# Four head pairs in the seven-product output projection, with weight sums made by accumulating transfers

## The chip, the cores and the metric

The kernel runs on one core of a Trainium2 chip. The metric is the device time of one execution in microseconds. The kernel before took 963.85 us (median of 3 runs, 963.8 to 965.16).

## The reference

One layer of a hybrid decoder, over 512 tokens and 16 learned meta tokens, model width 2048, all in float32:

```python
h = rms_norm(x, norm_w)
proj = (h @ w_in).astype(f32)
(dq, dk, dv, dz, db, da, gq, gk, gv, gz, gl, fq, fk, fv, fz, ff) = split_cols(proj)
...
o_dn = gated_head_norm(gated_delta_rule_chunked(...), dz, dn_norm_w)    # 6 heads x 128
o_gla = gated_head_norm(gla_chunked(...), gz, gla_norm_w)               # 5 heads x 128
o_fox = forgetting_attention(...) * silu(fz)                            # 5 heads x 128
o = jnp.concatenate([o_dn, o_gla, o_fox], axis=-1)[:, PAD:]
return x + o @ w_out          # then a final RMSNorm, meta tokens dropped
```

The output projection is `o @ w_out`: 512 tokens, 16 heads of 128 (eight head pairs `kp` 0 to 7), 2048 columns (four blocks `cc` of 512).

## The kernel before

Every matmul operand is split into a high and a low part, and a product is three matmuls: high by high, high by low, low by high. The program has three phases.

The first phase (about 93 to 490 us) is the input projection. Column blocks are taken in 18 pairs (`Pair`), and a pair is computed with seven products in place of eight (PE tile `px`). SyncE loads the raw weights `a`, VectorE makes their sums, ScalarE casts each operand to its high part `hp`, VectorE subtracts to get `lp`. Both have three buffers, and each operand of 128x1024 feeds 24 matmuls. Results that are needed later are spilled to DRAM. Beside it, the masks of DeltaNet (`an`, ten blocks) are loaded, cut with an AFFINE_SELECT on GpSimd and go into a triangular inverse (`inverse`, tile `ab`, on VectorE), whose result goes through a DRAM scratch `sc` and comes back as `xc`, transposed as `uc`, for the PE product `pm`.

The middle (490 to 817 us) runs the three mixers beside the rest of the input projection (`pbgz`, `pbfq`, `pbfz`, products of 512 columns) and the first part of the output projection (`po`). GLA's scores inside a chunk are `pss`: bursts of tiny matmuls of 64 and 32 rows, for the heads in pairs.

The last phase (817 us to the end) is the output projection. `PLAN` gives its order on PE. `OUT` holds plain products of head pairs 0 to 2. `Seven(cp)` does the column blocks 2cp and 2cp+1 with seven products for the head pairs in `ST`, here 3, 4 and 6 (PE tile `ps`). A set of seven products needs seven weight operands for each head pair: three raw quarters (numbers 1, 2, 3) and four sums (5, 7, 6, 4), and the same for the heads. `seven_raws` loads the quarters, `seven_sums` makes the sums on VectorE, `seven_operands` splits them into `wh` and `wl`, `seven_heads` does the heads, and `seven_adds` adds each product to the accumulator `acc` in SBUF. `late` holds the plain products of the head pairs not in `ST`, 5 and 7, for column blocks 0 to 2; `mm_last` takes the last column block, with head pairs 2, 5 and 7, one row block (128 tokens, `tb`) after the other, starting from `acc` (PE tile `pz`); each finished row block is normalised and sent out as 1 MB. The last row block goes in two halves. The order is late, Seven(0), late, Seven(1), late, last block.

What sets the order of the work is `Weave`, a list scheduler that runs when the kernel is built. Each piece of work is a generator with a priority; a cost model (`cost`) gives every instruction a duration, and the scheduler emits the instruction that could start first. That fixes the order of instructions on each engine. `BACK` says how far ahead of the model's clock of the DMA queues a load is asked for. The model changes no times on the chip, but every change in costs or work moves instructions everywhere behind it. SyncE issues nearly all transfers, in order; an instruction that waits holds what is behind it on its engine.

## Time and profile before

| | us |
|---|---|
| median of 3 runs | 963.85 |
| profiled execution | 968.62 |
| its span | 966.6 |
| TensorE busy in it | 949.7 |
| VectorE busy | 753.4 |
| ScalarE busy | 559.6 |
| GpSimd busy | 38.8 |

The profile shows one execution. Its span leaves out 2.0 us around the recorded instructions. A busy share is a mean over stages with different limits, so what a stage is worth is read from its own window and from the chain of work that ended last. PE records overlap, since matmuls are pipelined: a matmul of 128x512 has a duration of about 0.39 us and a start 0.23 us behind the one ahead of it. A wait "<-issue" is one for which the profile shows no other work or transfer that ended it.

### The profile page before, as it was taken

Reading aid. Unit: us, or ns where it says so; the run is one execution under the profiler, and the core shown is the slowest. Engines: PE = TensorE matmul, PEld = TensorE weight load, DVE = VectorE, ACT = ScalarE, POOL = GpSimd, SP = SyncE. Lnnn points to the kernel's source line nnn. Section 1 sums busy time; section 2 is a strip of 40 time slices with the busy share of each in tenths; the row PEclk is TensorE's granted clock in tenths of the full one; section 3 lists DMA queues with packets and bytes.
Section 4 is the critical chain, followed back from the end, with each engine's and each line's share of the span. In section 5 each row is a group of like instructions: output and inputs, shape, how many; then the busy total and the mean of one; then the engine's idle time right before and its main releaser. Section 6 shows DMA issues by size and latency. Waiting matters only on the chain.

```text
span 966.6 us, 18894 instructions
## 1 busy us (share of the span) xinstructions
PE 949.7 (98%) x7301; PEld 847.1 (88%) x7301; DVE 753.4 (78%) x1346; ACT 559.6 (58%) x1192; POOL 38.8 (4%) x86
## 2 busy tenths in 40 slices
PE   9999999999999999999999999989999999999996
PEld 7888999999999999999987897768787887888885
DVE  7986888888888788888983676866867976889874
ACT  7865566667756575654423775647555664335534
POOL 0000000000000000000000021001010100000000
PEclk9999999999999999999999999999999999999999
DMA  9933235426542545542188444324244246733105
GB/s 340 360 132 132 88 121 168 159 94 188 146 162 89 157 125 173 157 147 85 62 312 269 129 124 144 132 79 143 79 135 157 83 142 205 285 98 120 44 23 174
DMA packets 78894, 144.10 MB, mean 149 GB/s; under 512 B 14781, under 2 KB 35005, under 8 KB 78804
## 3 DMA queue, kind: packets, MB, share of 16 engines
q1 hardware_dynamic: 78516, 142.63, 44.8%
q8 instruction: 57, 0.93, 0.4%
q14 instruction: 33, 0.27, 0.1%
q10 hardware_dynamic: 288, 0.27, 0.1%
HBM read 119.26 MB, written 23.61 MB: 148 GB/s over the span
## 4 chain that ended last, share of the span: by engine, by line
PE 92%; DVE 3%; ACT 2%; DMA 2%; issue 1%; DVEq 0%; POOL 0%; SPq 0%; ACTq 0%; POOLq 0%
PE px L280 38%; PE po L280 11%; PE pz L280 6%; PE ps L280 6%; PE pbgz L280 5%; PE pbfz L280 5%; PE pbfq L280 4%; PE pbdz L280 2%; PE pks L280 2%; PE pfa L280 2%; PE pg L280 1%; PE pfw L280 1%; PE pss L280 1%; PE pbgq L280 1%; PE pgo L280 1%
## 5 line engine op out<-in xcount | busy, mean ns | idle before, releaser
L280 DVE SCALAR_TENSOR_TENSOR lp<-a,hp 128x1024 fp32r<-128x1024 f32 x90 | 110.7, 1230 | 37.1 <-ACT hp L280 36.6
L280 ACT CAST hp<-a 128x1024 fp32r<-128x1024 f32 x90 | 94.4, 1049 | 71.8 <-PE px L280 44.2
L280 PE MATMUL px<-xh,hp 128*128 128x264 f32 x432 | 123.9, 287 | 0.0
L280 PE MATMUL px<-xh,lp 128*128 128x264 f32 x432 | 122.7, 284 | 0.0
L280 PE MATMUL px<-xl,hp 128*128 128x264 f32 x432 | 122.7, 284 | 0.0
L280 PE MATMUL px<-tah,hp 128*128 128x264 f32 x288 | 84.0, 292 | 0.0
L280 PE MATMUL px<-tbh,lp 128*128 128x264 f32 x288 | 82.3, 286 | 0.0
L280 PE MATMUL px<-tbh,hp 128*128 128x264 f32 x288 | 82.1, 285 | 0.0
L280 PE MATMUL px<-tbl,hp 128*128 128x264 f32 x288 | 82.0, 285 | 0.0
L280 PE MATMUL px<-tah,lp 128*128 128x264 f32 x288 | 81.9, 284 | 0.0
L280 PE MATMUL px<-tal,hp 128*128 128x264 f32 x288 | 81.8, 284 | 0.0
L280 PEld LDWEIGHTS px<-xh,hp 128*128 128x128 f32 x432 | 81.4, 188 | 0.0
L280 PEld LDWEIGHTS px<-xl,hp 128*128 128x128 f32 x432 | 81.2, 188 | 0.0
L280 PEld LDWEIGHTS px<-xh,lp 128*128 128x128 f32 x432 | 81.2, 188 | 0.0
L280 PE MATMUL po<-ho,oh 128*128 128x512 f32 x136 | 54.6, 402 | 0.0
L280 PEld LDWEIGHTS px<-tbh,hp 128*128 128x128 f32 x288 | 54.3, 189 | 0.1
L280 PEld LDWEIGHTS px<-tah,hp 128*128 128x128 f32 x288 | 54.2, 188 | 0.1
L280 PEld LDWEIGHTS px<-tal,hp 128*128 128x128 f32 x288 | 54.3, 188 | 0.0
L280 PEld LDWEIGHTS px<-tah,lp 128*128 128x128 f32 x288 | 54.2, 188 | 0.0
L280 PEld LDWEIGHTS px<-tbl,hp 128*128 128x128 f32 x288 | 54.2, 188 | 0.0
L280 PEld LDWEIGHTS px<-tbh,lp 128*128 128x128 f32 x288 | 54.1, 188 | 0.0
L280 ACT CAST hp<-s 128x1024 fp32r<-128x1024 f32 x36 | 37.8, 1050 | 28.2 <-PE px L280 20.3
(416 smaller groups left out, 2603.2 us busy)
## 6 DMA issues: line engine op xcount, KB each, us to landing
a<-in_w_in SPq DMA_DIRECT2D x72, 512.0 KB, 3.8
o<-in_w_out SPq DMA_DIRECT2D x20, 512.0 KB, 3.2
rgz<-in_w_in SPq DMA_DIRECT2D x10, 512.0 KB, 5.8
rfq<-in_w_in SPq DMA_DIRECT2D x10, 512.0 KB, 4.4
rfz<-in_w_in SPq DMA_DIRECT2D x10, 512.0 KB
xs<-in_xT SPq DMA_DIRECT2D x16, 264.0 KB, 5.5
fraw<-in_w_first SPq DMA_DIRECT2D x16, 256.0 KB
xt<-in_xtok SPq DMA_DIRECT2D x8, 512.0 KB
```

The costliest lines, as they stand in the source:

```text
L280: self.pin(op.call(*op.a, **op.kw))
```

## The change

Head pair 7 goes from `late` into the seven products: `ST` is now `STK` = 3, 4, 6, 7, and `LATE` is 5 alone. The sums of the output weights are no longer made by VectorE. `out_sums` makes them in DRAM, in a scratch `osum`, during the first phase: one set (column pair, head pair) for every second `Pair`, eight sets in all. For each of a set's four sums SyncE copies one quarter of 256 KB from DRAM to DRAM, and GpSimd adds another to it with an accumulating transfer (numbers 5 and 7 add a quarter, 6 adds sum 5, 4 adds sum 6). Signs are moved to the head sums and to `seven_adds`, which now subtracts products 6 and 7. `seven_loads` loads 28 ready operands for each set of seven products, raw quarters from `w_out` and sums from `osum`, in the order in which they are used; the first six go into lent tiles (`kd`) as soon as these are free. In the scheduler, loads are asked for 1.5 us ahead in place of 3.0 once the model's clock is past 100 us, and GpSimd transfers have a cost of their own. `need`, `PLAN` and `late` follow from `STK`. `EARLY_KP` is empty, so its branches do nothing.

```diff
-AP, KA, BACK, XP, GAP = -0.2, 2, 3.0, 0.3, 0.1
+AP, KA, XP, GAP = -0.2, 2, 0.3, 0.1
+BACK, BT = (3.0, 1.5), 100.0
-WP = 1.0
+WP, AOP, HDP = 1.0, -0.6, 0.0
+EARLY_KP = ()
+STK, KOS, OS0, OSN, OSP = (3, 4, 6, 7), 3, 1, 2, 0.1
...
-        return 0.4, 0.0, b / 350e3
+        return (0.85, 0.0, b / 175e3) if key == "G" else (0.4, 0.0, b / 350e3)
...
-                            self.t.get("D", 0.0) - BACK if c[3][0].dma else 0.0) + c[1], c[2]
+                            self.t.get("D", 0.0) - BACK[self.t.get("P", 0.0) > BT] if c[3][0].dma else 0.0) + c[1], c[2]
...
-    ST = (3, 4, 6)
+    ST = STK
...
-    late = [[Out(cc, kp) for kp in LATE] for cc in range(3)]
-    PLAN = OUT + [late[0], SEV[0], late[1], SEV[1], late[2], [Out(3, kp, True) for kp in [2] + LATE]]
+    late = [[Out(cc, kp) for kp in LATE] for cc in range(3)] if LATE else []
+    PLAN = OUT + late[:1] + [SEV[0]] + late[1:2] + [SEV[1]] + late[2:] + [[Out(3, kp, True) for kp in [2] + LATE]]
...
-        for s in SEV:
-            W.go(seven_raws(s), -0.3, f"sraw{s.cp}")
-            for kp in ST:
-                W.go(seven_sums(s, kp), SSP, f"ssum{s.cp}{kp}")
+        W.go(seven_loads(), -0.3, "sloads")
...
-        yield VT(out=t[0][:, one_], in0=a[:, two], in1=b[:, two], op=ALU.add)
+        yield VT(out=t[0][:, one_], in0=a[:, two], in1=b[:, two], op=ALU.subtract)
...
-        yield VT(out=t[1][:, two], in0=b[:, one_], in1=t[0][:, two], op=ALU.subtract)
+        yield VT(out=t[1][:, two], in0=b[:, one_], in1=t[0][:, two], op=ALU.add)
...
+    osum = drp.tile([2, len(ST), P, 4, S], F32, name="osum")
+
+    def out_sums():
+        for i, (cp, kp) in enumerate((cp, kp) for cp in range(2) for kp in ST):
+            p, q = pairs[OS0 + OSN * i : OS0 + OSN * i + 2]
+            yield p.done[1]
+            t = osum[cp, ST.index(kp)]
+            (a, b), (c, d) = (tuple(w_out[2 * cp + n, kp][:, k * S : (k + 1) * S] for k in range(2)) for n in range(2))
+            for n, w in ((5, c), (7, d), (6, d), (4, b)):
+                yield SP.dma_start(out=t[:, SUMS.index(n)], in_=w)
+            for n, w, ev in ((5, a, p.done[6]), (7, c, p.done[7]), (6, t[:, SUMS.index(5)], q.done[1]),
+                             (4, t[:, SUMS.index(6)], q.done[6])):
+                yield ev
+                yield G.dma_start(out=t[:, SUMS.index(n)], in_=w, accum_op=ALU.add)
+        e_osum.set()
...
+    def seven_loads():
+        for s in SEV:
+            for i, (n, kp) in enumerate((n, kp) for n in ORDER for kp in ST):
+                    if i == 6:
+                        yield tuple(e_head[2 * kp] for kp in ST)
+                    t = yield Get((r_s, d_s) if i > 5 or s.cp else r_s, f"w{s.cp}{kp}{n}", (P, S), F32,
+                                  (0, KR) if i > 5 or s.cp else 0)
+                    sm = osum[s.cp, ST.index(kp)]
+                    raw = {1: (0, 0), 2: (0, 1), 3: (1, 1)}.get(n)
+                    src = w_out[2 * s.cp + raw[0], kp][:, raw[1] * S : (raw[1] + 1) * S] if raw else sm[:, SUMS.index(n)]
+                    yield SP.dma_start(out=t, in_=src)
+                    s.src[kp, n].set(t)
...
-            yield from add(tb + p, 2 * s.cp + c, ps[p])
+            yield from add(tb + p, 2 * s.cp + c, ps[p], ALU.subtract if n > 5 else ALU.add)
...
-            W.go(add_out(tb, cc, ps[tb]), -0.6 if cc == 2 else 0.0, f"add{tb}{cc}")
+            W.go(add_out(tb, cc, ps[tb]), AOP if cc != 2 else -0.6, f"add{tb}{cc}")
...
-    nc = bacc.Bacc("TRN2", target_bir_lowering=False, num_devices=1, dynamic_dma_scratch_size=256)
+    nc = bacc.Bacc("TRN2", target_bir_lowering=False, num_devices=1, dynamic_dma_scratch_size=1024)
```

In the last phase on PE the order of the stages is the same. Each `late` stage has 24 matmuls where it had 48, each set of seven products 168 where it had 126, and the last block 60 where it had 90 (its last row block in halves of 256 columns). In the first phase PE and VectorE keep their order but for a few rows.

On GpSimd the first rows behind its set-up were the masks of DeltaNet:

```order
L280 MEMSET misc_97 64x528
L280 AFFINE_SELECT an04_2415<-an04_2415 16x3x16
L280 AFFINE_SELECT an00_2588<-an00_2588 128x384
L280 AFFINE_SELECT an01_2691<-an01_2691 128x384
L280 AFFINE_SELECT an02_2858<-an02_2858 128x384
```

Now the accumulating transfers stand between them (`osum<-in_w_out` adds a quarter, `osum<-osum` adds a sum):

```order
L283 DMA osum<-in_w_out 128x512
L283 AFFINE_SELECT an_2437<-an_2437 16x3x16
L283 DMA osum<-in_w_out 128x512
L283 DMA osum<-osum 128x512
L283 AFFINE_SELECT an_2612<-an_2612 128x384
L283 DMA osum<-osum 128x512
L283 AFFINE_SELECT an_2726<-an_2726 128x384
```

So a mask is cut behind transfers that wait for SyncE's copies. The first accumulating transfer of a set stands directly ahead of a mask at four places.

On SyncE, in the middle, behind the store of the inverse's result (`sc<-ab`), the rows before were:

```order
L280 DMA sc_121<-ab 102x1024
L280 DMA an_5819<-ans_119 128x1536
L280 DMA rfq_5869<-in_w_in 128x1024
L280 DMA kT_5871<-spdk_1982 128x528
L280 DMA kT_5871<-spdk_2240 128x528
L280 DMA xc_5858<-sc_121 128x12x32
```

And now:

```order
L283 DMA sc_121<-ab 102x1024
L283 DMA rfq_5929<-in_w_in 128x1024
L283 DMA an_5917<-ans_119 128x1536
L283 DMA spgq_5968<-qgq_5965 128x512
L283 DMA xc_5939<-sc_121 128x12x32
```

The two loads of `kT` now come behind `xc`, and a store `spgq` ahead of it. On PE, `pm<-uc` stands three large matmuls (of 512 columns) earlier than before in the same product.

On PE, in GLA's first pair of heads, the second burst of `pss` (its last rows are those on `kx`) and the third (its first rows are those on `gkT`) stood like this before, with 15 large matmuls `pbfz` between them, of which three are shown at each end:

```order
L280 MATMUL pss_7464<-qx_6815,kx_6807 32x32
L280 MATMUL pfa_7282<-ident,fp_7321 128x128
L280 MATMUL pbfz_7476<-xh_149,hbfz_0_7351 128x512
L280 MATMUL pbfz_7476<-xl_150,hbfz_0_7351 128x512
L280 MATMUL pbfz_7476<-xh_149,lbfz_0_7352 128x512
...
L280 MATMUL pbfz_7476<-xh_254,hbfz_0_7351 128x512
L280 MATMUL pbfz_7476<-xl_255,hbfz_0_7351 128x512
L280 MATMUL pbfz_7476<-xh_254,lbfz_0_7352 128x512
L280 MATMUL pss_7571<-qx_6815,gkT_6850 32x32
```

Now three smaller matmuls of the attention (`pfa`) are all that lies between:

```order
L283 MATMUL pss_7522<-qx_6892,kx_6877 32x32
L283 MATMUL pfa_7538<-fk_7012,fq_7014 128x144
L283 MATMUL pfa_7539<-fk_7012,fq_7014 128x272
L283 MATMUL pfa_7540<-fk_7012,fq_7014 128x400
L283 MATMUL pss_7630<-qx_6892,gkT_6917 32x32
```

The large matmuls that were there have moved ahead of the second burst (24 now, 21 before) and behind the third. In the second pair of heads 15 large matmuls lie ahead of the last burst's four transposes and three behind them, where six lay in all.

## Prediction
> **What bounds the kernel now.** First I read the page's top lines, then the chain of work that ended last, from 817 us on, the last phase being where the change removes products.

> ```profile
> span 966.6 us, 18894 instructions
> PE 949.7 (98%) x7301; PEld 847.1 (88%) x7301; DVE 753.4 (78%) x1346; ACT 559.6 (58%) x1192; POOL 38.8 (4%) x86
> 817.41 44.48 PE po L280 x192
> 861.89 29.26 PE ps L280 x126
> 891.15 11.10 PE po L280 x48
> 902.25 29.20 PE ps L280 x126
> 931.45 11.10 PE po L280 x48
> 942.54 16.73 PE pz L280 x90
> ```

> TensorE is at work for 98% of the span, and the last phase is one unbroken run of matmuls: each row begins where the one ahead of it ended. So there a product left out is time gained, at 44.48 / 192 = 0.2317 us for a matmul of 512 columns. The view by windows shows the engines beside it:

> ```profile
> 93.00:200.00 107.00, 107.00 (x876) 106.41 (x875) 87.89 (x97) 63.88 (x133) 0.00 (x0) 1.00 0.39 132
> 200.00:300.00 100.00, 99.85 (x824) 98.96 (x824) 86.15 (x108) 67.00 (x130) 3.01 (x6) 1.00 0.49 148
> 400.00:480.00 80.00, 80.00 (x643) 79.30 (x642) 69.46 (x92) 39.75 (x79) 2.51 (x3) 1.00 0.34 107
> 862.00:891.00 29.00, 29.00 (x127) 23.36 (x126) 25.64 (x41) 14.21 (x26) 0.00 (x0) 1.00 0.38 127
> ```

> The columns are the window, its length, busy time and instructions of PE, weight load, VectorE, ScalarE and GpSimd, then the granted clock, the DMA share and GB/s. In the first phase PE never pauses at full clock, VectorE works 82 to 87% of the time, and the DMA engines are taken 0.34 to 0.49. In the seven-product stage VectorE works 25.64 of 29.00 us, yet PE waits for nothing. What PE does wait for lies between 490 and 817 us:

> ```profile
> PE pss L280 <- issue: 3.1, 3, 2.2
> PE pkd L280 <- DVE gst L280: 1.2, 2, 0.8
> PE pm L280 <- DVE uc L280: 1.1, 1, 1.1
> ```

> (The columns are the total, the times, and the longest.) So three things decide: products removed at the end, whether the first phase stays covered, and what a new order makes of the middle.

> **The last phase: -2.78 us on PE.** Head pair 7 leaves three stages of plain products (24 matmuls each) and the last block (24 of 512 columns in width): 96 leave. It joins two sets of seven products, six matmuls to each: 84 come. Net 12 x 0.2317 = **-2.78 us**. Nothing covers these matmuls, so all of it shows unless something else becomes late.

> VectorE loses the weight sums, 24 operations like these:

> ```profile
> L280 DVE SCALAR_TENSOR_TENSOR wl<-kd,wh 128x512 fp32r<-128x512 f32 x21 | 13.9, 687 | 1.6 <-ACT wh L280 1.1 <-issue 0.5
> L280 DVE SCALAR_TENSOR_TENSOR w<-w,w 128x512 f32<-128x512 f32 x5 | 3.4, 687 | 0.1
> kd<-in_w_out SPq DMA_DIRECT2D x12, 256.0 KB, 6.0
> ```

> That is 24 x 0.687 = 16.5 us of VectorE beside a PE that did not wait, so I count 0 for it. The new operands must come at one per six matmuls, 1.39 us; VectorE needs 0.687 for each and 256 KB per 1.39 us is 189 GB/s, under the 341 to 371 that the output reaches further down. A landing of 6.0 us is covered if loads are asked for five operands ahead; the first six have lent buffers early. 0 again.

> **The tail: +0.6 us.** The last block has four row blocks, each normalised and sent out as 1 MB. Their 18 matmuls (4.17 us) become 12 (2.78 us).

> ```profile
> 946.79 0.60 ACT L280 ACTIVATE sqf<-pz 128x512 f32<-128x512 f32 x1 [2.71 <-PE pz L280]
> 948.08 1.34 ACT L280 ACTIVATE acc<-acc,frs 128x512 f32<-128x512 f32 x2
> 959.30 0.38 ACT L280 ACTIVATE sqf<-pz 128x256 f32<-128x256 f32 x1 [1.25 <-PE pz L280]
> 950.00:952.00 2.00, 2.00 (x10) 1.64 (x9) 0.00 (x0) 1.04 (x4) 0.00 (x0) 1.00 1.09 341
> 962.00:964.00 2.00, 0.00 (x0) 0.00 (x0) 0.00 (x0) 0.00 (x0) 0.00 (x0) 1.00 1.04 371
> ```

> 1 MB at 341 to 371 GB/s takes 3.1 to 2.8 us, about 3.0, and before each block had 4.17. At 2.78 a block transfers wait for each other: 0.22 per block, three times, 0.66. ScalarE needs about 2.6 us per block (946.79 to 949.42), still under 2.78, but its two half squares in the last block may queue 0.4 behind that, partly the same delay. Ends: 0 (the last pieces overlap) and +1.1; I take **+0.6**, near the 0.66.

> **The first phase: 0.** Eight sets of sums come in, each four copies of 256 KB inside DRAM (SP) and four accumulating ones (GpSimd): 16.8 MB written and more read, which no row of before shows. If each moved byte costs as in the 148 GB/s row (0.49 / 148), 8 sets over some 330 us add 0.15 to 0.3 to a share of 0.34 to 0.49: room is left. On the path it counts only when an operand comes late:

> ```profile
> a<-in_w_in SPq DMA_DIRECT2D x63, 512.0 KB, 3.6
> ACT hp L280 <- PE px L280: 64.5, 51, 2.2
> DVE s L280 <- DMA a<-in_w_in: 4.9, 3, 1.9
> ```

> The first gives the landing of an input-weight load; the others are waits. ScalarE mostly waits for PE to free an operand, so producers run ahead. An operand feeds 24 matmuls, 24 x 107.00 / 876 = 2.93 us; with three buffers two are ahead, 5.9 us. Waits of 1.9 us for a load did not reach PE. A load queued behind one set's 1 MB lands about 3.0 us later and is hidden. Bounds: below, nothing can be gained, PE being full; above, the +6.0 of the third rival. I take the lower end, since even the row with waits left PE at 100%.

> [...]

> **The middle: +0.1 us, the least certain term.** The scheduler put other work between the same steps, as the order shows.

> ```profile
> 631.18 1.35 PE L280 MATMUL pss<-qx,kx 64*32 64x32 f32 x128
> 637.53 1.07 PE L280 MATMUL pss<-qx,kx 64*32 64x32 f32 x103
> 639.28 0.33 PE L280 MATMUL pss<-qx,kx 64*32 64x32 f32 x25 [0.68 <-issue]
> 646.43 0.58 PE L280 MATMUL pss<-gqT,gkT 64*32 64x32 f32 x43 [2.23 <-issue]
> 645.00:647.00 2.00, 0.57 (x44) 0.53 (x44) 0.00 (x0) 0.00 (x0) 0.00 (x0) 1.00 0.00 0
> 647.00:650.00 3.00, 3.00 (x10) 2.42 (x10) 2.23 (x11) 1.44 (x5) 0.00 (x0) 0.50 0.02 5
> 711.77 0.72 PE L280 MATMUL pss<-qx,gkT 64*32 64x32 f32 x62
> 713.09 0.30 PE L280 MATMUL pss<-gqT,gkT 64*32 64x32 f32 x17 [0.17 <-issue]
> ```

> The intra-chunk scores come in bursts of 128 tiny matmuls, 1.3 us each; twice in the first pair of GLA heads PE waited for nothing but its own instructions (0.68 and 2.23, while DMA stood still), and from 647 us ran at clock 0.50 for 3.0 us, costing 1.5. In the second pair, with 1.9 us of other work between two bursts, the wait was 0.17. Before, 15 large matmuls (3.5 us) lay between the second and third burst of the first pair; now three small ones do. If instructions arrive at the second pair's pace, the missing 1.9 us turn into a wait: 0.17 + 1.9 = 2.1 against 2.9 before, -0.8. If they arrive at the first pair's pace, all 3.5 show: +3.5. Between ends that far apart I stay near the second pair's row and take +0.6. In the second pair 15 large matmuls now lie where 6 did: -0.2.

> The 1.5 of the slow clock stays in the sum as it is. [...]

> ```profile
> 506.35 0.29 SPq L280 DMA_DIRECT2D sc<-ab  x1
> 514.31 0.37 SPq L280 DMA_DIRECT2D xc<-sc  x1
> 519.67 0.58 DVE L280 STREAM_TRANSPOSE uc<-xc 128x384 f32<-128x384 f32 x1 [4.62 <-DMA xc<-sc]
> 520.31 0.95 PE L280 MATMUL pm<-uc,an 32*32 32x32 f32 x48 [1.12 <-DVE uc L280]
> ```

> After the DeltaNet inverse its result goes through DRAM, 7.96 us out and 5.36 back, and PE waited 1.12 for it. Now two loads of 264 KB are issued behind xc instead of ahead of it (-1.1 at best), while PE comes three matmuls earlier (+0.7 at worst). I take -0.3. Together +0.6 - 0.2 - 0.3 = **+0.1**.

> **Sum.** -2.78 + 0.6 + 0 + 0.1 = -2.08 us: 968.62 becomes 966.54, -0.21%. The profiled execution is 0.5% above the median of 963.85; scaled to that, 963.85 x 966.54 / 968.62 = **961.8 us**. A measurement of this kernel can tell 0.2% (1.9 us) from no change, so the forecast lies right beside that bound.

> **The rivals.**
> - *The tail and the bursts give it back* (within 0.2%). Output takes +1.1 and the bursts +1.5: -2.78 + 1.1 + 1.5 - 0.5 = -0.7, 963.2 us. For it: 2.78 is already below 3.0. Against: the last pieces of 128 to 256 KB overlap.
> - *Instruction waits grow* (slower). Back-to-back bursts at the first pair's pace: +3.5 for the lost cover and a second stretch at clock 0.50, +1.5. -2.78 + 0.6 + 5.0 - 0.5 = +2.3, 966.1 us. It decides once the wait in the first pair exceeds the 2.9 us of before by 4.6 us or so, clock included. Against it: the wait of 0.17 in the second pair.
> - *GpSimd's queue holds the masks* (slower). The accumulating transfer of a set stands ahead of a DeltaNet mask (`an`) on GpSimd at four places, and waits for its copy, issued shortly before. VectorE uses the mask in a fixed order between the operands. A mask waits for its own loads (taken as the 3.6 above); PE starves when the copy lands over 3.6 + 5.9 = 9.5 us after issue. At 11 us: 4 x 1.5 = +6.0, 967.7 us; the sum turns slower by more than 0.2% at 10.5. Against it: the longest landing here was sc's 7.96.
> - *The stall dissolves* (faster by more). Later asking leaves the DMA queues free at the bursts: -2.9 and -1.5 of clock, 968.62 - 2.78 + 0.6 - 4.4 - 0.5 = 961.5, scaled 956.8 us.

> **Chances.** Forecast 0.45 (with some 1 us about it, so 0.3 of it under the bound, 0.15 within), give-back 0.17, instruction waits 0.17, GpSimd's queue 0.08, stall gone 0.13. Faster by over 0.2%: 0.3 + 0.13 = 0.43; within: 0.15 + 0.17 = 0.32; slower: 0.25. The range leaves out the far half of the last two rivals' cases: 957.5 to 967.0. The forecast's own is 960.8 to 962.8.

> **What would show it.** Right: po rows of 24 matmuls and ps rows of 168 without a pause, the last pz row with 60, PE at 1.00 in the windows of 93 to 480 us, the output's share near 1 from the first block on, and the 7.3 us from the last matmul to the end growing by about 0.6. Wrong: a wait of PE for px's operands in the first phase; an `an` of GpSimd over 5 us late; <-issue waits above 5 us in total or more windows at clock 0.50; PE waiting for wh or wl in the seven-product stages.

## The result and the profile after

| | before | changed |
|---|---|---|
| median, us | 964.48 (963.8 to 965.16, 4 runs) | 973.94 (971.35 to 977.23, 4 runs) |
| ratio | | 1.010, interval 1.0061 to 1.0139 |
| profiled execution, us | 968.62 | 971.76 |

The change makes the kernel about 1% slower, where 0.2% faster was forecast. The profiled execution of before, 968.62, lies above all four of these runs; why executions of one kernel differ by some 5 us comes out below.

The chain of work of the changed kernel, its last phase:

```profile
822.93 38.98 PE po L283 x168
861.91 38.92 PE ps L283 x168
900.83 5.56 PE po L283 x24
906.39 38.94 PE ps L283 x168
945.33 5.57 PE po L283 x24
950.89 8.35 PE pz L283 x36
```

The late stages have 24 matmuls, the sets of seven products 168, without a gap, as forecast. (The chain shows only 36 of the last block's matmuls, since it goes over to ScalarE at 959.24 us.) But the phase begins at 822.93 in place of 817.41. Four markers place what happened in between (starts of the same matmuls in both traces, read from the timelines of PE):

| us | before | changed | difference on the way from the marker above |
|---|---|---|---|
| first matmul behind the first phase (`pbgq`) | 476.13 | 475.64 | -0.49 |
| start of the last phase (`po`) | 817.41 | 822.93 | +6.01 |
| last matmul of the last block | 958.98 | 961.78 | -2.72 |
| end of the span | 966.6 | 970.0 | +0.60 |

So the first phase is covered, the last phase brings 2.72 us, the tail takes 0.60, and the middle loses 6.0 us. The first phase by windows of the changed kernel (columns as before):

```profile
93.00:200.00 107.00, 107.00 (x876) 106.53 (x876) 88.06 (x97) 64.08 (x133) 7.64 (x9) 1.00 0.62 179
200.00:300.00 100.00, 99.87 (x827) 99.37 (x826) 86.47 (x108) 69.75 (x133) 10.37 (x15) 1.00 0.74 195
400.00:480.00 80.00, 80.00 (x641) 79.22 (x640) 69.34 (x92) 39.94 (x80) 6.62 (x8) 1.00 0.49 137
```

The DMA share rises by 0.15 to 0.25, and PE has no pause. The DMA issues of the first phase (the last column is the landing), and on GpSimd's timeline a mask that came when it did before and the two that did not:

```profile
a<-in_w_in SPq DMA_DIRECT2D x63, 512.0 KB, 6.4
osum<-in_w_out POOLq DMA_DIRECT2D x16, 256.0 KB, 5.7
osum<-osum POOLq DMA_DIRECT2D x16, 256.0 KB, 7.0
213.32 0.41 POOL L283 TENSOR_SCALAR_AFFINE_SELECT an<-an 16x48 f32<-16x48 f32 x1 [14.63 <-DMA an<-gd]
255.40 0.52 POOL L283 TENSOR_SCALAR_AFFINE_SELECT an<-an 128x384 f32<-128x384 f32 x1 [14.04 <-DMA an<-spdk]
272.96 0.73 POOL L283 TENSOR_SCALAR_AFFINE_SELECT an<-an 128x384 f32<-128x384 f32 x1 [8.65 <-DMA an<-spdk]
```

An input weight lands in 6.4 us (3.6 before): the 2.8 us more are about half of the 5.9 that producers were ahead, and PE waits for none. Eight of the ten masks are cut within 1.1 us of where they were before (the first at 213.81 there). Two come 5.7 and 15.4 us later (249.66 and 257.60 there); both wait for their own loads, not for the copies, and cost PE nothing, since it has no pause. Where the middle loses, the waits of PE show it:

```profile
PE pss L283 <- issue: 5.1, 3, 2.6
PE pfw L283 <- DVE ml L283: 2.0, 3, 1.3
PE pkd L283 <- DVE gst L283: 1.9, 2, 1.1
PE pvf L283 <- DMA fv<-spfv: 0.7, 1, 0.7
PE pm L283 <- DVE uc L283: 0.7, 1, 0.7
```

The waits in the score bursts (`pss`) grow from 3.1 to 5.1 us. The timeline of PE with them, and windows around:

```profile
646.24 0.59 PE L283 MATMUL pss<-gqT,gkT 64*32 64x32 f32 x36 [2.64 <-issue]
713.23 0.28 PE L283 MATMUL pss<-qx,kx 64*32 64x32 f32 x11 [0.98 <-issue]
720.73 0.43 PE L283 MATMUL pss<-gqT,gkT 64*32 64x32 f32 x34 [1.49 <-issue]
648.00:650.00 2.00, 2.00 (x7) 1.55 (x6) 1.90 (x11) 1.80 (x7) 0.00 (x0) 0.53 0.01 4
722.00:724.00 2.00, 2.00 (x6) 1.52 (x5) 0.58 (x3) 1.13 (x3) 0.00 (x0) 0.50 0.00 0
```

The first pair of heads waits 2.64 us in one burst (0.68 and 2.23 before, in two). New is the second pair: 0.98 and 1.49, and a second stretch at clock 0.50 behind them. The waits for issue are 2.0 us longer, the new stretch of half clock costs some 1.6 (matmuls of 512 columns start 0.43 us apart, not 0.23), and the other waits of the middle add up to 7.8 us against 4.9, so 2.9 more: 6.5 in all, against the 6.0 of the markers. The other waits are for VectorE, ScalarE and loads; nearly half of the loss is theirs.

In the tail, SyncE is at its outputs from 955.56 on; from 957 to 967 us the DMA share is 0.99 to 1.09 in every microsecond, past the last matmul too:

```profile
962.00:964.00 2.00, 0.06 (x1) 0.00 (x0) 1.36 (x6) 1.49 (x7) 0.00 (x0) 1.00 1.02 316
964.00:966.00 2.00, 0.00 (x0) 0.00 (x0) 1.02 (x3) 0.34 (x1) 0.00 (x0) 1.00 1.06 391
966.00:968.00 2.00, 0.00 (x0) 0.00 (x0) 0.00 (x0) 0.00 (x0) 0.00 (x0) 0.83 0.96 349
```

Before, the share fell to between 0.29 and 0.76 in the pauses between blocks; now the four blocks follow each other without one, which fits the 0.60.

### The profile page after: what moved, and what is told of

It reads as the page before. It is cut to its first block, busy times and chain, and to the rows that moved or that the text cites. A ratio compares the mean times of both kernels' runs of the same rounds, so it can differ in the third digit from the quotient of the medians.

```text
span 970.0 us, 19077 instructions
## 1 busy us (share of the span) xinstructions
PE 947.7 (98%) x7283; PEld 844.5 (87%) x7283; DVE 750.5 (77%) x1337; ACT 569.6 (59%) x1205; POOL 67.1 (7%) x118
## 4 chain that ended last, share of the span: by engine, by line
PE 90%; DVE 3%; ACT 3%; issue 1%; DMA 1%; POOL 0%; SPq 0%; DVEq 0%; ACTq 0%; POOLq 0%
PE px L283 38%; PE po L283 9%; PE ps L283 8%; PE pz L283 5%; PE pbfq L283 5%; PE pbfz L283 5%; PE pbgz L283 4%; PE pbdz L283 2%; PE pbgq L283 2%; PE pg L283 1%; PE pss L283 1%; PE pfa L283 1%; PE pks L283 1%; PE pfw L283 1%; PE pgo L283 1%
## 5 line engine op out<-in xcount | busy, mean ns | idle before, releaser
L283 DVE SCALAR_TENSOR_TENSOR lp<-s,hp 128x1024 fp32r<-128x1024 f32 x36 | 44.0, 1221 | 7.9 <-ACT hp L283 7.9
## 6 DMA issues: line engine op xcount, KB each, us to landing
a<-in_w_in SPq DMA_DIRECT2D x72, 512.0 KB, 5.7
osum<-in_w_out SPq DMA_DIRECT2D x32, 256.0 KB, 5.0
o<-in_w_out SPq DMA_DIRECT2D x16, 512.0 KB, 3.5
kd<-osum SPq DMA_DIRECT2D x25, 256.0 KB, 3.8
kd<-in_w_out SPq DMA_DIRECT2D x21, 256.0 KB, 4.2
rgz<-in_w_in SPq DMA_DIRECT2D x10, 512.0 KB
rfq<-in_w_in SPq DMA_DIRECT2D x10, 512.0 KB, 3.2
rfz<-in_w_in SPq DMA_DIRECT2D x10, 512.0 KB, 3.2
```

The lines of the kernel that those rows point to most:

```text
L283: self.pin(op.call(*op.a, **op.kw))
```

## The experiments

### Which part of the change costs (e1, e2, e5, e6)

```diff
-BACK, BT = (3.0, 1.5), 100.0
+BACK, BT = (3.0, 3.0), 100.0     e1, in the changed kernel
+BACK, BT = (3.0, 1.5), 500.0     e5, in the changed kernel
+BACK, BT = (1.5, 3.0), 500.0     e6, in the changed kernel
+BACK, BT = (3.0, 1.5), 100.0     e2, in the kernel before
```

(The words behind a line say which run it belongs to. e2 also takes over the line of the change that uses `BT`.)

> The whole change, but loads are asked for 3.0 us ahead all through, as before (BACK = 3.0, 3.0). With that the order of PE in the middle is that of the kernel before. Theory A (the loss is in the order of the middle: bursts of tiny score matmuls whose instructions come late, and the half clock behind them): waits for issue about 3 us and one stretch at clock 0.50 as before, the last phase 2 to 3 us shorter, 960.5 to 963.5 us. Theory B (the loss is the transfers and the accumulation themselves, or the operands of four head pairs): as the changed kernel, 971 to 977 us.

> The kernel before, with nothing but the loads asked for later (BACK = 3.0, 1.5 past 100 us). Theory A: another order of the middle, with bursts in other places; some 2 to 6 us of waits for issue, 963 to 970 us, the loss in those waits and the clock. Theory C (loads asked for later arrive late): slower by 5 us or more with waits of PE for DMA, above all vgv, fv and kT, and few more for issue. Theory B: no change, 963 to 965 us.

> The whole change, with loads asked for later only past 500 us of the model's clock (BACK = 3.0, 1.5; BT = 500). PE's order is that of the changed kernel but for some rows of the first phase. If the loss is made behind 500 us, be it by the order of the middle or by loads asked for late there: 970 to 978 us, with waits for issue of 4 to 6 us and two stretches at clock 0.50. If it is made by later loads in the first phase: 961 to 964 us.

> The other half: loads asked for later from the start (1.5 us) up to 500 us of the model's clock, as before (3.0 us) behind it. The middle has the order of the kernel before. Loss made behind 500 us: 961 to 965 us, as run e1. Loss made in the first phase: 970 us and more.

| run | median, us | ratio to before, interval |
|---|---|---|
| e1 | 963.41 | 0.9983, 0.9959 to 1.0006 |
| e6 | 962.66 | 0.9983, 0.9958 to 1.0008 |
| e5 | 971.53 | 1.0062, 1.0036 to 1.0088 |
| e2 | 974.83 | 1.0100, 1.0059 to 1.0141 |

Without the later asking behind 500 us the change gives about the -0.2% that was forecast, though the intervals include no change. The whole loss comes with loads asked for later past 500 us of the model's clock, where the first phase is over. e1's and e6's middle has the order of the kernel before but for some rows, e5's that of the changed kernel, with waits for issue of 4.5 us in its profile. Of the two stretches at half clock that were expected in e5 its profile shows none, and it took 969.98 us: the loss does not need them.

e2 fits none of the theories whole: it is slower by 1%, but the waits in its profile are not for instructions, and of the longest five only one is for a transfer:

```profile
PE po L281 <- DVE a L281: 1.7, 1, 1.7
PE pvgv L281 <- DMA vgv<-spgv: 1.6, 1, 1.6
PE ps L281 <- DVE wl L281: 1.5, 3, 1.0
PE pm L281 <- DVE uc L281: 1.3, 1, 1.3
PE po L281 <- DVE an L281: 1.2, 1, 1.2
```

The kernel before, asked to load later, gets yet another order of its middle, with waits of its own (and its seven products wait for weights, 1.5 us, which the changed kernel's do not). Behind the 1.7 us for VectorE's `a` PE runs at half clock too, at 0.50 from 800 to 802 us.

### The bursts with a quarter of their instructions (e3, e4)

In the bursts of the levels 16 to 0, three of four matmuls are left out and the fourth covers their columns; the scheduler still counts all of them, so the order is kept. The scores are others.

```diff
-mm.append(PE.matmul(pss[e][o0 : o0 + n, off + b * n : off + b * n + n], kx[rr, k0 : k0 + n],
-                    qx[rr, q0 : q0 + n], start=True, stop=True))
+wide = n if s > 16 or b else 4 * n
+mm.append(PE.matmul(pss[e][o0 : o0 + n, off + b * n : off + b * n + wide], kx[rr, k0 : k0 + n],
+                    qx[rr, q0 : q0 + wide], start=True, stop=True))
+mm[-1].skip = s <= 16 and b > 0
...
-self.pin(op.call(*op.a, **op.kw))
+if not op.skip:
+    self.pin(op.call(*op.a, **op.kw))
```

> The changed kernel with the same order; in each burst of the scores on levels 16 to 0, one matmul of four is issued, four times as wide, so three of four instructions are gone and the scores are others. Theory A: no wait for issue above 0.3 us and no stretch at clock 0.50 in the middle; against the changed kernel 9 to 14 us are gone (5.1 of waits, 3.3 of clock, 4 of the bursts), 960 to 964 us. Theories B and C: only the 4 us of the bursts are gone, 967 to 972 us.

> The kernel before with the same edit of the bursts (three of four of their instructions left out, other scores). Theory A: 3.1 us of waits, 1.5 of clock and 4 of bursts gone, 954 to 957 us, so that the changed kernel with this edit is at most 3 us above it or below it. Theories B and C: the distance between the two stays at 9 us.

The changed kernel goes to 963.02 us (961.51 to 972.09), the kernel before to 961.37 (959.83 to 961.99). In both profiles no wait for issue is left and no stretch of half clock in the middle, though the DMA share ahead of e3's third bursts is 0.95 and 0.89. The distance between the kernels shrinks from 9.5 us to 1.65: most of the loss hangs on the instructions of the bursts. Not all, for the changed kernel has 2.2 us less to do; the other waits of PE add up to 11.7 us in e3's profile and 5.3 in e4's. e4 came out 4.4 us above what was expected. That fits if most executions of before lack its waits: 16 of the 25 beside these runs lie between 962.2 and 965.9 us, and the profiled one, 968.62, was of the others.

### Transfers beside a burst, in an order that is kept (e9, e13, e14), and the changed kernel again (e15)

e1 with stores of 256 KB to a scratch that nothing reads. The scheduler counts them as taking no time, so PE's order is e1's row for row; e13 and e14 go through the four sources twice.

```diff
+if p == 1 and group[0] == 1:      e9: four, ahead of the second pair's last burst
+if p == 1 and group[0] == 4:      e13: eight, ahead of the burst before it
+if p == 0 and group[0] == 4:      e14: eight, in the first pair
+    extra = []
+    for q, src in enumerate((ops[group[0]][2], pair[1][:, NM:], pair[2][:, NM:], pair[3][:, NM:])):
+        o = SP.dma_start(out=drp.tile([P, S], F32, name=f"xtra{q}"), in_=src)
+        o.dur = o.lat = o.dma = 0.0
+        extra.append(o)
+    yield extra
 yield mm
```

> Run e1 (the change, loads asked for as before) with four more stores of 256 KB to a DRAM scratch, issued by SyncE as soon as the operands of the second pair's last score burst are written; nothing reads them, and PE's order is row for row that of e1. In e1 this burst waited 0.53 us for its instructions, with a DMA share of 0.31 in the 3 us ahead. If instructions come late because they queue behind transfers: 1.5 us or more of wait for issue at this burst, often a stretch at clock 0.50 behind it, 2 to 4 us above e1, 964.5 to 968 us, and few executions below 963. If the order of PE alone makes the waits: 0.2 to 0.7 us there, time as e1, 962 to 964 us.

> Run e1 with eight stores of 256 KB to a DRAM scratch, issued when the operands of the second pair's second burst are written, so that 2 MB move between the second and the third burst (e9's four came only during the third: 0.74 in it, 0.35 ahead). PE's order is that of e1. If instructions that are fetched behind transfers come late: DMA share above 0.8 in the 3 us ahead of the third burst, a wait for issue there of 1.5 us or more, often a stretch at clock 0.50, 965 to 969 us, and hardly an execution below 963. If the transfers do not matter: wait there 0.2 to 0.6 us, 961.5 to 964 us.

> The same eight stores between the second and the third burst of the first pair, where a share of 0.7 was measured already, with a wait of 1.96 us in e1's profile and none in e9's. If more transfers make the wait certain: nearly all executions at 966 to 969 us, wait at the third burst above 1.5 us. If it is left to chance as before: both kinds, 961.5 to 963 and 966 to 969 us.

> The changed kernel as it is, on the chip of these runs, for the spread of its executions. If its waits for instructions are certain in its order (shares of 0.88 and more ahead of two bursts): no execution below 968 us, median 970 to 975, clock 0.992 to 0.997. If they are left to chance: some executions at 962 to 965 us.

e9 missed: its transfers came during the burst, not ahead of it (share 0.35 ahead, 0.74 in it), and the burst waited 0.26 us; 963.23 us (one of its ten executions took 3276 us, for which no run shows a cause). e13 put them ahead. First e1's third burst of the second pair with the window ahead of it, then e13's, and what followed:

```profile
712.85 0.30 PE L283 MATMUL pss<-gqT,gkT 64*32 64x32 f32 x17 [0.53 <-issue]
708.20:711.20 3.00, 3.00 (x114) 2.41 (x108) 2.64 (x9) 1.48 (x4) 2.10 (x6) 1.00 0.31 112
```

```profile
709.54 0.30 PE L283 MATMUL pss<-gqT,gkT 64*32 64x32 f32 x17 [1.62 <-issue]
703.80:706.80 3.00, 3.00 (x135) 2.43 (x109) 2.72 (x9) 1.46 (x4) 2.17 (x6) 1.00 0.97 365
710.00:712.00 2.00, 2.00 (x6) 1.61 (x6) 1.55 (x5) 0.95 (x2) 0.00 (x0) 0.50 0.34 125
```

With the same PE order, a DMA share of 0.97 ahead of the burst goes with a wait of 1.62 us, where 0.31 went with 0.53, and a stretch at half clock follows (one profiled execution of each). The time is 964.52 us, a little under the 965 to 969 that was expected, but its executions spread from 962.32 to 967.56 where eight of e1's ten lie from 961.7 to 962.7 or from 967.5 to 968.3; two of them lie below 963, where hardly one was expected. In e14 it stayed a matter of chance: five executions from 963.12 to 964.3, five from 967.89 to 970.87, and the profiled one, with a share of 1.02 ahead, did not wait there.

In the changed kernel it is no matter of chance (e15): all ten executions of the changed kernel lie between 969.03 and 982.37 us, median 971.46 (ratio 1.0068, 1.0031 to 1.0106). Its waits stand where they stood:

```profile
646.74 0.52 PE L283 MATMUL pss<-gqT,gkT 64*32 64x32 f32 x36 [2.36 <-issue]
714.28 0.28 PE L283 MATMUL pss<-qx,kx 64*32 64x32 f32 x11 [0.99 <-issue]
721.96 0.43 PE L283 MATMUL pss<-gqT,gkT 64*32 64x32 f32 x34 [1.67 <-issue]
```

All profiles that have the order of before or of the changed kernel and its bursts whole, for the third burst of each pair: the DMA share in the 3 us ahead of it, and its wait for issue. The shares are worked out as in the windows above.

| | first pair: share, wait us | second pair: share, wait us |
|---|---|---|
| before | 0.76, 2.23 | 0.32, 0.17 |
| e1 | 0.74, 1.96 | 0.31, 0.53 |
| e6 | 0.91, 1.68 | 0.21, 0.52 |
| e9 | 0.68, 0.00 | 0.35, 0.26 |
| e14 | 1.02, 0.00 | 0.28, 0.52 |
| e12 | 0.60, 0.00 | 0.20, 0.52 |
| e13 | 0.71, 0.00 | 0.97, 1.62 |
| changed | 0.98, 2.64 | 0.89, 1.49 |
| e5 | 1.03, 2.09 | 0.88, 1.39 |
| e15 | 0.92, 2.36 | 0.90, 1.67 |

In the second pair the wait goes with the share: 0.17 to 0.53 below 0.4, 1.39 to 1.67 from 0.88 on. In the first pair a share of 0.6 to 1.0 goes with a wait or with none. The second bursts do not follow the share at all: 0.67 to 0.95 us of wait at shares of 0.21 to 0.30 in before, e1 and e6.

The traces show what PE waited for. They hold the packets of every DMA queue, those of PE's instructions too (changed kernel; the columns are packets, MB, share):

```profile
q8 instruction: 57, 0.93, 0.4%
```

Each of the 57 packets has 16 KB. PE's 7283 matmuls and as many weight loads make about 256 instructions to a packet, and in e3, with 6563 of each, there are 51 packets. Counted along PE's recorded instructions, all 24 waits for issue inside bursts, in the ten profiles that have any, stand a multiple of 256 apart, to within one: PE waits where one packet's instructions, a block, end and the next block begins. None of the 17 profiles has PE begin a block earlier than 1.21 us after that block's packet has landed, and each of the 24 waits ended 1.23 to 1.56 us after. So what decided in these profiles is when the packet came, and how long PE was busy with the block ahead of it. All times are in us:

| wait looked at | PE's own time for the block ahead | from its begin to the start of the next packet | DMA share until then | from landing to the next block | wait |
|---|---|---|---|---|---|
| first pair, second burst, before | 6.32 | 4.57 | 0.35 | 1.55 | 0.68 |
| the same, e9 | 6.08 | 0.96 | 0.00 | 4.24 | none |
| first pair, third burst, before | 4.92 | 4.72 | 0.74 | 1.56 | 2.23 |
| the same, e14 | 4.84 | 2.29 | 1.03 | 1.66 | none |
| the same, changed | 3.04 | 3.28 | 0.93 | 1.49 | 2.64 |
| second pair, third burst, e1 | 3.29 | 1.25 | 0.11 | 1.26 | 0.53 |
| the same, e13 | 3.30 | 2.70 | 0.99 | 1.28 | 1.62 |
| the same, changed | 6.01 | 5.17 | 0.65 | 1.41 | 1.49 |

(PE's own time is from the begin of one block to that of the next, less the wait. A packet itself took 0.9 to 1.3 us in these rows.) At the second and third bursts of all ten profiles a packet starts at most 1.3 us after the block ahead of its own while the DMA share is below 0.2, and up to 5.4 us after it (e15) beside transfers. The block ahead of the second pair's third burst keeps PE busy for only 3.3 us, in the order of before; that is less than the packet's start, the packet and the 1.2 to 1.6 us behind it add up to even beside few transfers, so the six profiles with a share of 0.20 to 0.35 there all show a small wait, 0.17 to 0.53 us. e13's transfers make it long.

This also shows what was left to chance in the first pair. In e9, e12, e13 and e14 the packet for the second burst starts 0.8 to 1.0 us after the block ahead has begun, and a load `rgz` moves behind it; in before, e1 and e6 the packet starts 4.5 to 4.9 us after, behind that load. It is a close race: in e1 and e13 the block begins at 632.67 and 632.66 us and the load is issued at 633.13 in both, and the packet starts at 637.21 and at 633.64. Where the packet comes late the second burst waits, the block ahead of the third begins later, its packet falls behind further transfers, and the third burst waits too. In these seven profiles the two waits come together or not at all. e14's transfers came after that was decided, and the packet for its third burst still arrived in time. In the changed order the large matmuls between the bursts are gone, PE is busy with the block for only 3.0 us, and the third burst waits in all three profiles (changed, e5, e15).

### Other places for the bursts (e7, e8, e10, e11)

e7 and e8 give the bursts out in halves of 64 matmuls with large matmuls between (in e1 and in the changed kernel); e10 and e11 hold a burst back until the scheduler's own clock of the DMA queues has come down (likewise).

```diff
-yield mm                                                    e7, e8
+for i in range(0, len(mm), 32):
+    yield mm[i:i + 32]
...
+c[4] = max(c[4], self.burst + 1.5)                          e7, e8: 1.5 us behind the last piece
+c[4] = max(c[4], min(self.t.get("D", 0.0) + 0.0, r + 8.0))  e10, e11: r is when it could start
```

> The change with loads asked for as before (run e1), and each burst of 64 score matmuls given out in pieces of 32 that start at least 1.5 us of the model's clock after the piece ahead of them, so that large matmuls come between. Nothing is left out. If instructions that come late in the bursts are the cost: no wait for issue above 0.3 us, no stretch at clock 0.50, 957 to 961 us, below both kernels. If the waits have another cause than the density of instructions (the transfers beside them): waits for issue of 2 us or more stay, 962 to 966 us.

> The changed kernel, loads asked for 1.5 us ahead, with the same pieces of 32. Theory A (bursts and clock make the loss): 958 to 963 us, no wait for issue above 0.3 us, no stretch at 0.50. If loads that are asked for later are late by themselves: 966 to 972 us, with waits of PE for DMA (fv, gv, kT, weights) of 3 us or more in all, and no wait for issue.

> The change with loads asked for as before, and a rule in the scheduler: a score burst is given out only when the model's clock of the DMA queues has fallen back to PE's (or 8 us after it could start). The order of the middle becomes another one. If transfers beside the bursts are the cost and the model's clock is good enough: DMA shares below 0.5 ahead of the bursts, waits for issue below 1 us in all, 960 to 963 us with hardly an execution above 966. If the new order costs other waits, as in e7: 965 to 970 us without waits for issue.

> The changed kernel (loads asked for 1.5 us ahead past 100) with the same rule for the bursts. If its loss is the bursts beside late transfers: waits for issue below 1 us, 961 to 965 us. If asking late costs by itself, as run e2 of the kernel before suggests (972.8 us and more without a wait for issue in its profile): 968 us or more, with the loss in waits of PE for VectorE and DMA.

| run | median, us | ratio to before, interval | waits for issue |
|---|---|---|---|
| e7 | 969.36 | 1.0040, 1.0018 to 1.0061 | none |
| e8 | 968.87 | 1.0047, 1.0020 to 1.0073 | none |
| e10 | 963.09 | 0.9968, 0.9941 to 0.9995 | none |
| e11 | 964.63 | 0.9982, 0.9960 to 1.0003 | none in a burst |

The halves do away with the waits for instructions, as expected, and win nothing (957 to 961 us were expected for e7, 958 to 963 for e8): the middle gets a new order with other waits. In e7's profile PE waits 1.4 us for `wl` and 1.5 for `fp`, which e1 does not show. e10 and e11 do better: with the bursts moved to other places, the kernel that asks for its loads late costs 964.6 and not 971 to 974. So loads asked for late need not cost 1% by themselves; what counts is their place beside the bursts, in this order. But the rule moves much else too, and the DMA shares ahead of e10's bursts are still 0.45 to 0.77 in five of six, so it doesn't work through quiet queues alone. e10 is the one kernel with all of the change's products that is below the kernel before by more than its interval.

### The seven products with three head pairs (e12)

```diff
-BACK, BT = (3.0, 1.5), 100.0
+BACK, BT = (3.0, 3.0), 100.0
...
-STK, KOS, OS0, OSN, OSP = (3, 4, 6, 7), 3, 1, 2, 0.1
+STK, KOS, OS0, OSN, OSP = (3, 4, 6), 3, 1, 2, 0.1
```

> Run e1 with three head pairs in the seven products, as before (STK = 3, 4, 6): weight sums by accumulating transfers, but PE's work is that of the kernel before. The order of the middle is that of before. If the gain of e1 is the 12 matmuls of 512 columns (2.78 us) less 0.6 in the tail: 964 to 966 us, 2 us above e1 and the same as the kernel before. If sums made ahead by transfers give or cost something by themselves: away from that by more than 1 us.

964.09 us (963.61 to 964.93), between e9's 963.23 on the same chip and the 965.28 of before (ratio 0.9974, 0.9951 to 0.9997). The lowest executions are 1.1 us apart (962.54 in e9, 963.61), half of the 2.2 that 12 matmuls less 0.6 should bring; that much is within what these runs scatter. The sums made ahead cost nothing that these runs can tell.

## Why the prediction was wrong

The steps that held: the matmuls (-2.78 forecast, -2.72 between the markers), the tail (+0.6; +0.60), the first phase at 0 (-0.49; part of it lies before 93 us, where the changed kernel was 0.1 ahead already), and the room that it was given: beside SyncE's copies and GpSimd's sums an input weight landed in 6.4 us in place of 3.6 and the DMA share rose to 0.74 at most in the windows shown. The rival of GpSimd's queue is out: copies landed in 5.0 us (median), and PE waited for nothing in the first phase, though two masks were over 5 us late. The inverse (-0.3): PE's wait for `uc` fell from 1.12 to 0.7.

**The step that failed is the middle, "+0.1 us, the least certain term".** It was off by 5.9 us in the profiled execution. By its own terms: the bursts of the first pair, +0.6 forecast, came to -0.3 (2.91 us of wait before, 2.64 now); those of the second pair, -0.2 forecast, to +2.3 of waits and 1.6 of half clock; the inverse, -0.3, to -0.4; and waits that had no term, to +3.3. Two of its signs of being wrong came true there: over 5 us of waits for issue, and a second stretch at half clock. Three errors stand in it.

First, the waits were put down to how close two bursts lie in PE's order. For the first pair that was near the truth. The second pair, with 18 large matmuls ahead of its last burst where six lay, was counted at -0.2; it is there that the changed kernel waits 2.5 us and runs at half clock. The order of PE showed the distance but not what else moves then. PE had 6.0 us of work ahead of that burst, enough had its packet started as early as in e1 (1.25 us after the block ahead began, and the next block came after 3.8); it started 5.17 us after. The timeline of SyncE shows what was there by then: a second load, a store and another load, which in e1 come only behind this burst.

```profile
713.56 0.33 SPq L283 DMA_DIRECT2D rfq<-in_w_in  x1
715.15 0.33 SPq L283 DMA_DIRECT2D spgz<-zgz  x1
715.53 0.42 SPq L283 DMA_DIRECT2D fk<-spfk  x1
```

They raise the share ahead of the burst to 0.89, and e13 shows that transfers alone, with PE's order kept, hold a packet back (2.70 us in place of 1.25). So asking for loads later was not a detail of the scheduler: it moved transfers next to the bursts. The rival "instruction waits grow", at +5.0 on top and with a chance of 0.17, had longer waits and a second stretch at half clock, but from lost cover in the first pair, whose waits did not grow.

Second, the profiled execution of before was taken for the usual one. Its 2.9 us of waits in the first pair and 1.5 of half clock were in the sum on both sides. No profile shows before without them, but in nearly the same order e9 and e14 have none in that pair and took 962.71 and 963.86 us, e1 has both and took 967.48; and 62 of the 103 executions of before beside the experiments lie below 966.2 us. So it is likely, though not shown, that more executions of before lack them than have them. A kernel in which they come every time loses them whole against such an execution. An estimate: 5.1 of waits, 1.5 to 3.1 of half clock and 2.9 of other waits, less the 2.6 that the first phase, the last phase and the tail bring, are 6.9 to 8.5 us; the profiled execution of the changed kernel lies 7.3 us above the median of before. On the chip of e15, where 13 of 25 executions of before took 967 us or more, the medians are only 4.4 us apart. What makes some executions of the changed kernel take 976 to 982 us was not profiled.

Third, that a reordered middle also changes waits for VectorE, ScalarE and loads (7.8 against 4.9 us) had no term at all. e2 and e7 are slower than before with such waits and none for instructions.

A burst is 256 instructions in 1.3 us, weight loads counted, and the three bursts of the changed kernel that waited did so for 0.98 to 2.64 us. On the clock, a wait of 1.49 us in the changed kernel was followed by half clock, one of 1.67 in e15 and one of 2.09 in e5 were not; no run here shows what decides it.

What stays open: what holds a packet back, in e1's first pair even for 1.2 us after the load ahead of it was through; and how much of e2's loss is due to its order and how much to the loads.

## What to carry to other kernels

Work taken off a full engine came out to a tenth of a microsecond here (2.72 of 2.78); what the scheduler moved on the way cost more than twice that (6.0), so a change in its rules is to be timed apart from the work that it comes with. Where tiny instructions come in dense bursts, see how long PE is busy with each 256 instructions, weight loads counted: here PE waited 0.17 to 0.53 us behind a block of 3.3 us even beside few transfers (DMA share 0.20 to 0.35). Then look at the transfers in the microseconds ahead, not at PE's order alone (in one order, 0.53 us of wait at a share of 0.31 and 1.62 at 0.97). Before a wait of the profile goes into a sum, see whether the other executions have it.
